# Convolution taps from PSUM, the triangles' inverse in PSUM, first values by segment, and x·sigmoid(x) as one activation

## The chip, the core and the metric

The kernel runs on one core of a Trainium2 chip. A core has five engines that run side by side, each through its own instructions in a fixed order: TensorE (PE) multiplies matrices, VectorE (DVE) and GpSimd (POOL) do elementwise work, ScalarE (ACT) applies functions, SyncE (SP) issues transfers. Engines wait for each other by semaphores. Data lie in SBUF (128 partitions) and in PSUM, whose banks hold 512 fp32 values a partition and take TensorE's results. The metric is the device time of one run in microseconds (us), lower is better.

## The reference

Two attention layers run over 1024 tokens and 256 context tokens, width 1024; a mixer block with an MLP runs on the 1024 tokens. Cut to what the change touches:

```python
# first block, each layer: modulation and gate
shift, scale, gate = split(silu(c) @ w_mod + b_mod, 3)
attn = rms_norm(o, subln_g) * (1 - lam_init)
x = x + gate * (concat([fourier_mix(a_in), pool_mix(b_in), attn]) * silu(g)) @ w_out

# second block: three branches from one projection of h
q_a = silu(a_q); o_a = gated_linear_attention(q_a, k_a, a_i, log_f_a)
qkv = silu(causal_short_conv(c_qkv, gdn_conv))      # 4 taps along time
m = eye(64) + where(strict, beta * (k @ k.T) * decay, 0)
sol = triangular_solve(m, rhs)                      # chunks of 64, unit diagonal
y = g0 * y_a + g1 * y_b + g2 * y_c;  x = x + rmsnorm(y @ w_out)
x = x + rmsnorm(square(relu(h @ w_up)) @ w_down)
```

## The kernel before

Tokens are cut into segments 0 and 1 (512 tokens each) and 2 (the context, 256). Every fp32 product is made of three matmuls on a high and a low part of both operands (lines 199 to 201, names `pp`, `h_hi`, `h_lo`, `whi`, `wlo`). A weight arrives as `wraw` by a DMA on SP's queue, ACT copies its high part (`whi`, line 177), POOL subtracts for the low part (`wlo`, line 178); there are 6 buffers of such pairs. A framework orders the instructions of every engine before the run and puts in the semaphores; the code's order sets priorities.

In layer 0 the modulation of the later steps (`mod`) is made while the Fourier projection runs: DVE adds up `w_mod` rows into `modacc` (lines 431, 433), TensorE sums over partitions into `modps` (line 437). The Fourier mixing itself goes through small products `mps` and `uvps`, DVE's additions into `uv` (line 1070) and the matmuls `eps`.

The mixer works on four pairs of heads p = 0 to 3 in pieces, whose code order stands in the tables MIX_FIRST, MIX and MIX_LAST: Av, Aq, Af, Ag project the first branch (`proj_tm` and `proj_fm`; each result goes to one of three `pp` banks and is evacuated by a callback), GA and GB are the two linear attentions, NA, NB, NC the output norms (line 1345), gA, gB, gC the gates `gs` (lines 1294 to 1299), Ck, Cq and Cv the convolved projections of the third branch (`conv`), I the triangles' inverse (`m_I`), U, Y, D what follows from it. `m_I` inverts 32 by 32 triangles, one per partition, by 31 steps on DVE: step i multiplies the rows known so far with a column (`tr`, line 1705) and sums (`ur`, line 1706). TensorE's `yp` product (line 1729) waits for the inverse. In `conv` ACT copies the product to `cv` and its scaled copy to `cvo` (lines 1602, 1604), DVE adds three shifted taps (line 1606), ACT takes the sigmoid (line 1608) and POOL multiplies (line 1609). Buffers named by `wt` (4 KB) come from a ring of 16, those by `wh` (2 KB) from a ring of 8.

Of the kernel before, what the change touches and what calls it, by code (L numbers as in the profile page):

```python
# [39 lines left out]
def shape_tables():  # L40
# [79 lines left out]
class Model:  # L120
# [130 lines left out]
    def setup(self):  # L251
# [5 lines left out]
        self.half = cp.tile([128, 1], F32, name="half")  # L257
        nc.gpsimd.memset(self.half, -0.5)
# [49 lines left out]
    def block1(self):  # L308
# [33 lines left out]
        sg = b1.tile([128, 8, 2], F32, name="sg")  # L342
# [68 lines left out]
    def mod(self, l, c0, sb, tp, bufs, add, tag="modps", depth=1):  # L411
# [4 lines left out]
        ps = tp.tile([128, 512], F32, tag=tag, name="modps", bufs=depth)  # L416
        pt = (ps if add else tp.tile([128, 512], F32, tag=tag, name="modpt", bufs=depth))[:, 0:8].rearrange("p (t two) -> p t two", two=2)
        if add:
            acc = sb.tile([128, 2, 512], F32, tag="modacc", name="modacc", bufs=2)
        for i in range(4):  # L420
            w = sb.tile([128, 2, 512], F32, tag="wmod", name="wmod", bufs=bufs)
            nc.sync.dma_start(out=w, in_=self.a["w_mod"][l, i * 256:(i + 1) * 256, c0:c0 + 512].rearrange("(k p) n -> p k n", p=128))
            for j in range(2):
# [4 lines left out]
                for c in range(2):  # L428
# [91 lines left out]
    def layer(self, l):  # L520
# [14 lines left out]

        def more(n=1):
# [85 lines left out]
        with ExitStack() as es:  # L622
            self.pp = self.pool("pp", bufs=4, space=PSUM, ctx=es)
            self.norm_pools(es, side="right")
            yp = self.pool("yp", ctx=es)
            for group in [(g,) for g in segs]:
                y = {}
                for g in group:
                    y[g] = [Tiles(e + t) for e, t in zip(early, self.load_y(yp, y_d, g, range(4, 8)))] if g == 0 else [Tiles(t) for t in self.load_y(yp, y_d, g, range(8))]
# [19 lines left out]
    def load_y(self, yp, y_d, g, ks, n=8, m=3):  # L649
# [4 lines left out]
        for k in ks:  # L654
            st = yp.tile([128, 512], F32, tag="yst", name="yst", bufs=m)[:, :ln]
# [73 lines left out]
    def attention(self, l, es, ak, ps_s, qk_d, v, g_d, y_d, upd):  # L729
# [139 lines left out]
        def step(i):  # L869
# [70 lines left out]
            def llast():  # L940
# [222 lines left out]
    def mixer(self, es):  # L1163
# [10 lines left out]
        self.g2_d = self.grid("g2_d", [128, 8, 128], 3, 8)  # L1174
        self.tri = mp.tile([128, 2, 128], F32, name="tri")
# [804 lines left out]
```

## Time and profile before

| what | value |
|---|---|
| median of 3 runs | 4307.32 us (4303.39 to 4315.31) |
| the profiled execution | 4301.6 us, span 4299.8 us |
| mean granted TensorE clock | 0.958 |
| PE busy | 3997.2 us, 93% of the span |
| DVE, ACT, POOL busy | 1926.8, 1528.3, 2005.0 us |

The span runs from the first to the last instruction. A share of busy time is a mean over stages with different limits: attention layer 0 lies before about 895 us, layer 1 before 1549 us, the mixer from 1563 to about 3500 us with four like periods of some 464 us, the MLP behind it. A busy PE at a lower granted clock takes longer for the same matmul.

### The profile page before, as it was taken

Reading aid. Unit: us, or ns where it says so; the run is one execution under the profiler, and the core shown is the slowest. Engines: PE = TensorE matmul, PEld = TensorE weight load, DVE = VectorE, ACT = ScalarE, POOL = GpSimd, SP = SyncE. Lnnn points to the kernel's source line nnn. Section 1 sums busy time; section 2 is a strip of 40 time slices with the busy share of each in tenths; the row PEclk is TensorE's granted clock in tenths of the full one; section 3 lists DMA queues with packets and bytes.
Section 4 is the critical chain, followed back from the end, with each engine's and each line's share of the span. In section 5 each row is a group of like instructions: output and inputs, shape, how many; then the busy total and the mean of one; then the engine's idle time right before and its main releaser. Section 6 shows DMA issues by size and latency. Waiting matters only on the chain.

```text
span 4299.8 us, 71521 instructions
## 1 busy us (share of the span) xinstructions
PE 3997.2 (93%) x28027; PEld 3445.3 (80%) x28027; DVE 1926.8 (45%) x3252; ACT 1528.3 (36%) x3256; POOL 2005.0 (47%) x2306
## 2 busy tenths in 40 slices
PE   6989999999999989999989898989989989999998
PEld 3878877788788778879879897979868877888886
DVE  3467376555347433464255623482258355122121
ACT  4221366433247433441224222341224134243332
POOL 2523122454312335564366536563566465445444
PEclk9989999999999999899999999999989889999999
DMA  6556321646422431222112221122112334334332
GB/s 217 166 176 201 124 83 46 202 146 177 164 76 75 135 89 43 70 67 66 56 53 61 65 66 55 46 68 68 50 41 62 94 120 159 96 98 132 99 96 83
DMA packets 372510, 429.20 MB, mean 100 GB/s; under 512 B 56743, under 2 KB 273341, under 8 KB 371917
## 3 DMA queue, kind: packets, MB, share of 16 engines
q1 hardware_dynamic: 283632, 294.60, 22.9%
q10 hardware_dynamic: 78620, 93.33, 6.8%
q0 software_dynamic: 9920, 36.70, 2.6%
q8 instruction: 220, 3.60, 0.3%
q14 instruction: 118, 0.96, 0.1%
HBM read 328.88 MB, written 95.64 MB: 99 GB/s over the span
## 4 chain that ended last, share of the span: by engine, by line
PE 57%; DVE 8%; POOL 4%; issue 4%; DMA 3%; ACT 2%; ACTq 1%; SPq 0%; DVEq 0%; POOLq 0%
PE pp L199 12%; PE pp L201 12%; PE pp L200 12%; PE dn L200 3%; PE dn L201 3%; PE dn L199 3%; DVE tr L1705 2%; PE o_ps L831 2%; DVE cvo L1606 1%; PE lv L1459 1%; PE t_ps L815 1%; DVE ur L1706 1%; POOL wlo L178 1%; PE s_ps L767 1%; PE s_ps L766 1%
## 5 line engine op out<-in xcount | busy, mean ns | idle before, releaser
L178 POOL TENSOR_TENSOR wlo<-wraw,whi 128x512 fp32r<-128x512 f32 x582 | 796.7, 1387 | 892.2 <-ACT whi L177 766.4
L199 PE MATMUL pp<-h_hi,whi 128*128 128x512 f32 (+1 forms) x2112 | 821.8, 390 | 34.6 <-ACT cvo L1604 16.3
L200 PE MATMUL pp<-h_lo,whi 128*128 128x512 f32 (+1 forms) x2112 | 815.0, 387 | 0.9 <-POOL h_lo L502 0.9
L201 PE MATMUL pp<-h_hi,wlo 128*128 128x512 f32 (+1 forms) x2112 | 811.2, 386 | 2.5 <-POOL wlo L178 2.5
L199 PE MATMUL pp<-whi,h_hi 128*128 128x256 f32 x2368 | 687.9, 292 | 35.5 <-ACT v L1431 14.0
L200 PE MATMUL pp<-wlo,h_hi 128*128 128x256 f32 x2368 | 687.0, 291 | 4.8 <-POOL wlo L178 4.8
L201 PE MATMUL pp<-whi,h_lo 128*128 128x256 f32 x2368 | 686.4, 290 | 0.0
L199 PEld LDWEIGHTS pp<-h_hi,whi 128*128 128x128 f32 x2112 | 404.5, 192 | 115.7 <-ACT cvo L1604 17.9
L199 PEld LDWEIGHTS pp<-whi,h_hi 128*128 128x128 f32 x2368 | 462.6, 196 | 40.1 <-ACT v L1431 14.2
L177 ACT ACTIVATE whi<-wraw 128x512 fp32r<-128x512 f32 x582 | 357.7, 625 | 374.0 <-PE pp L200 171.1
L200 PEld LDWEIGHTS pp<-wlo,h_hi 128*128 128x128 f32 x2368 | 464.0, 196 | 8.5 <-POOL wlo L178 6.5
L201 PEld LDWEIGHTS pp<-h_hi,wlo 128*128 128x128 f32 x2112 | 403.7, 191 | 81.7 <-POOL wlo L178 3.8
L200 PEld LDWEIGHTS pp<-h_lo,whi 128*128 128x128 f32 x2112 | 404.0, 191 | 76.1 <-POOL h_lo L502 1.2
L201 PEld LDWEIGHTS pp<-whi,h_lo 128*128 128x128 f32 x2368 | 462.5, 196 | 2.1
L787 DVE TENSOR_REDUCE mb<-s_ps 128x1 f32<-128x1280 f32 (+1 forms) x144 | 195.8, 1370 | 130.5 <-PE s_ps L767 128.4
L189 POOL TENSOR_TENSOR wlo<-wraw,whi 128x512 fp32r<-128x512 f32 x128 | 166.4, 1304 | 163.0 <-ACT whi L188 162.7
L200 PE MATMUL dn<-wlo,hid_hi 128*128 128x512 f32 x512 | 200.1, 391 | 0.0
L199 PE MATMUL dn<-whi,hid_hi 128*128 128x512 f32 x512 | 200.0, 391 | 0.0
L201 PE MATMUL dn<-whi,hid_lo 128*128 128x512 f32 x512 | 199.4, 391 | 0.0
L1606 DVE SCALAR_TENSOR_TENSOR cvo<-cv,vec,cvo 128x512 f32<-128x512 f32 x144 | 149.5, 1038 | 81.9 <-ACT cvo L1604 63.3
L796 ACT ACTIVATE p<-s_ps,mb 128x1280 f32<-128x1280 f32 x128 | 170.1, 1329 | 37.7 <-DVE mb L787 34.4
L1297 POOL TENSOR_TENSOR gs<-gs 128x256 f32<-128x256 f32 x96 | 76.2, 794 | 228.8 <-DVE gs L1296 226.5
(460 smaller groups left out, 7243.7 us busy)
## 6 DMA issues: line engine op xcount, KB each, us to landing
wraw<-in_w_in_dram SPq DMA_DIRECT2D x208, 256.0 KB
wraw<-in_w_up_dram SPq DMA_DIRECT2D x128, 256.0 KB
wraw<-in_w_down_dram SPq DMA_DIRECT2D x128, 256.0 KB
wraw<-in_w_out_dram SPq DMA_DIRECT2D x112, 256.0 KB
wraw<-in_w_in_dram SPq DMA_DIRECT2D x224, 128.0 KB
wmod<-in_w_mod_dram SPq DMA_DIRECT2D x48, 512.0 KB
qk<-qk_d POOLq DMA_DIRECT2D x16, 1280.0 KB, 6.7
g_d<-gs ACTq DMA_DIRECT2D x96, 128.0 KB
```

The source lines that it names most:

```text
L177: nc.scalar.activation(out=hi[:, :k, :o], in_=raw[:, :k, :o], func=AF.Copy)
L178: nc.gpsimd.tensor_tensor(out=lo[:, :k, :o], in0=raw[:, :k, :o], in1=hi[:, :k, :o].bitcast(F32), op=SUB)
L189: nc.gpsimd.tensor_tensor(out=lo, in0=raw, in1=hi.bitcast(F32), op=SUB)
L199: mm(ps, a[0], b[0], start=first, stop=False)
L200: mm(ps, a[0], b[1], start=False, stop=False)
L201: mm(ps, a[1], b[0], start=False, stop=last)
L787: V.tensor_reduce(out=b, in_=u.ps[m], axis=AX.X, op=MAX, negate=True)
L796: nc.scalar.activation(out=u.p[m], in_=u.ps[m], func=AF.Exp, bias=u.b[m], accum_out=u.s[m])
L831: mm(t.o_ps, v[k][:, t.hd * 128:t.hd * 128 + 128], t.parts[k // 4][:, k % 4], start=k == 0, stop=k == 9)
L1297: nc.gpsimd.tensor_tensor(out=t, in0=t, in1=sg[:, :, 128:256], op=MUL)
L1606: nc.vector.scalar_tensor_tensor(out=o, in0=r[:, 1 + j:513 + j], scalar=tap(j, f), in1=o, op0=MUL, op1=ADD)
L1705: V.tensor_tensor(out=tr[:, :n, :m], in0=ur[:, :n, :m], in1=mr[:, :m, i].unsqueeze(1).to_broadcast([128, n, m]), op=MUL)
```

## The change

Five edits. (1) `conv` keeps the product in its `pp` bank: the three shifted taps on DVE read the bank itself, an ACT copy `c_e` saves the last three columns of segment 0, and three narrow DVE taps add them at the start of segment 1. (2) The inverse `ur` lies in a PSUM bank, `tr` in a 2 KB buffer, and ACT copies the finished inverse to `us`, from which SP stores it; DVE instead of POOL sets its start values. (3) The first two projections of the mixer, Av and Aq of p = 0, are coded by segment (both load their weights twice: 8 more loads), and the mixer's constants are coded behind them. (4) Where sigmoid and a multiplication made x·sigmoid(x) (conv, Aq, gates of the layers, `sc`), one Silu activation stands. The gain `sub_gain` moves from the gate into `norm_apply`. (5) `mod` is cut in two stages: the sums on DVE, and TensorE's product with what follows it; `more` finishes one group's second stage when it starts the next group.

By the orders of both kernels, DVE loses 16 products of Aq, 40 of the gates and 2 of `sc`; its 144 taps of 128x512 become 144 on 511, 510 or 509 columns that read PSUM, and 72 of 1 to 3 columns. ACT loses 48 `cv` copies and 48 sigmoids, and gains 48 Silu, 24 `c_e`, 4 `us`, 8 `whi` and 19 table loads (36 before, 55 now). POOL loses 48 products and 48 small copies or memsets, and gains 8 `wlo`. PE's matmuls are as many as before.

```diff
-MIX_FIRST = "Av+"
+MIX_FIRST = "Av Aq Av Aq"
...
-        self.half = cp.tile([128, 1], F32, name="half")
-        nc.gpsimd.memset(self.half, -0.5)
+        self.half = self.ind[:, 4:5]
...
         for j, nm in enumerate(("c", "c_ctx")):
-            nc.scalar.activation(out=sg[:, :, j], in_=self.vec[nm], func=AF.Sigmoid)
-            nc.vector.tensor_tensor(out=self.sc[:, :, j], in0=sg[:, :, j], in1=self.vec[nm], op=MUL)
+            nc.scalar.activation(out=self.sc[:, :, j], in_=self.vec[nm], func=AF.Silu)
...
+    def mod_stages(self, l, c0, sb, tp, bufs, add, tag="modps", depth=1):
...
+        yield
+        pt = tp.tile([128, 512], F32, tag=tag, name="modpt", bufs=depth)[:, 0:8].rearrange("p (t two) -> p t two", two=2)
         if add:
...
         def more(n=1):
-            for c in left[:n]:
-                with self.tc.issue_after(self.mark.ins):
-                    self.mod(*c, mw, tp, 5, True, "fo", 5)
-            del left[:n]
+            for _ in range(n):
+
+                while open_:
+                    next(open_.pop(), 0)
+                if left:
+                    with self.tc.issue_after(self.mark.ins):
+                        open_.append(self.mod_stages(*left.pop(0), mw, tp, 5, True, "fo", 5))
+                        next(open_[0])
...
                 def evac_g(f, g, ps):
                     off, ln = SEG[g]
                     sg = gp.tile([128, 512], F32, tag="sg", name="sg", bufs=2)[:, :ln]
-                    nc.scalar.activation(out=sg, in_=ps, func=AF.Sigmoid)
-                    if wb < 2:
-                        nc.vector.tensor_tensor(out=sg, in0=sg, in1=ps, op=MUL)
-                    else:
-                        nc.vector.scalar_tensor_tensor(out=sg, in0=sg, scalar=self.sub_gain[:, l:l + 1], in1=ps, op0=MUL, op1=MUL)
+                    nc.scalar.activation(out=sg, in_=ps, func=AF.Silu)
...
-            yp = self.pool("yp", ctx=es)
+
+            ysp, xnp, yp = (self.pool(n, ctx=es) for n in ("ys", "xn", "yp"))
...
-        self.nc.vector.tensor_tensor(out=o, in0=o, in1=ps[:, 2:4].rearrange("p a b -> p (a b)"), op=MUL)
+        self.nc.vector.scalar_tensor_tensor(out=o, in0=o, scalar=gain, in1=ps[:, 2:4].rearrange("p a b -> p (a b)"), op0=MUL, op1=MUL)
...
+        for name in MIX_FIRST.split():
+            self.piece("m_", name, 0)
+        self.mixer_constants(mp)
...
         def ev(f, g, ps):
             s = slice(512 * g, 512 * g + 512)
-            nc.scalar.activation(out=q[f][:, s], in_=ps, func=AF.Sigmoid)
-            nc.vector.tensor_tensor(out=q[f][:, s], in0=q[f][:, s], in1=ps, op=MUL)
-
-        self.proj_fm([self.W[:, 256 * p:256 * p + 256]], self.h, (0, 1), ev)
+            nc.scalar.activation(out=q[f][:, s], in_=ps, func=AF.Silu)
+
+        if p == 0:
+            return self.by_segment(lambda segs: self.proj_fm(cols, self.h, segs, ev))
+        self.proj_fm(cols, self.h, (0, 1), ev)
+
+    def by_segment(self, f):
+
+        for g in (0, 1):
+            f((g,))
+            yield
...
         def evac(f, g, ps):
-            r = raw[f, g] = self.wh("cv", [128, 516])
-            if g == 0:
-                nc.gpsimd.memset(r[:, 0:4], 0.0)
-            else:
-                nc.gpsimd.tensor_copy(out=r[:, 0:4], in_=raw[f, 0][:, 512:516])
-            nc.scalar.activation(out=r[:, 4:], in_=ps, func=AF.Copy)
             o = out[f][:, 512 * g:512 * g + 512]
             nc.scalar.activation(out=o, in_=ps, func=AF.Copy, scale=tap(3, f))
-            for j in range(3):
-                nc.vector.scalar_tensor_tensor(out=o, in0=r[:, 1 + j:513 + j], scalar=tap(j, f), in1=o, op0=MUL, op1=ADD)
-            sg = self.wh("sg")
-            nc.scalar.activation(out=sg, in_=o, func=AF.Sigmoid)
-            nc.gpsimd.tensor_tensor(out=o, in0=o, in1=sg, op=MUL)
+            if g == 0:
+                last[f] = self.st("c_e", [128, 3], bufs=2)
+                nc.scalar.activation(out=last[f], in_=ps[:, 509:512], func=AF.Copy)
+            for d in range(1, 4):
+                V.scalar_tensor_tensor(out=o[:, d:], in0=ps[:, 0:512 - d], scalar=tap(3 - d, f), in1=o[:, d:], op0=MUL, op1=ADD)
+            if g:
+                for d in range(1, 4):
+                    V.scalar_tensor_tensor(out=o[:, :d], in0=last[f][:, 3 - d:], scalar=tap(3 - d, f), in1=o[:, :d], op0=MUL, op1=ADD)
+            nc.scalar.activation(out=o, in_=o, func=AF.Silu)
...
         mr = self.wt("mr", [128, 32, 32])
-        ur = self.wt("ur")[:, :512].rearrange("p (j i) -> p j i", i=32)
-        tr = self.wt("tr")[:, :512].rearrange("p (j i) -> p j i", i=32)
-        G.memset(ur, 0.0)
+        ur = self.op_.tile([128, 16, 32], F32, tag="o", name="ur")
+        us = self.wh("us", [128, 16, 32])
+        tr = self.wh("tr", [128, 16, 32])
+        V.memset(ur, 0.0)
...
+        nc.scalar.activation(out=us, in_=ur, func=AF.Copy)
         for e in range(2):
-            nc.sync.dma_start(out=ud.rearrange("h c b (j two) i -> two (h c b) j i", two=2)[e], in_=ur[64 * e:64 * e + 64])
+            nc.sync.dma_start(out=ud.rearrange("h c b (j two) i -> two (h c b) j i", two=2)[e], in_=us[64 * e:64 * e + 64])
...
-                    xt = gp.tile([128, D], F32, tag="fx", name="fx", bufs=4)
+                    xt = (self.wt("y0") if t % 2 else gp.tile([128, D], F32, tag="fx", name="fx", bufs=2))
```

**Layer 0, behind the gate's projection, PE.** Before; `modps` is the modulation, `mps` and `uvps` the Fourier part:

```order
L437 MATMUL modps<-ind,modacc 128x1 x4
L1060 MATMUL mps<-mid,wc 128x2
L1066 MATMUL uvps<-wc,eo 128x128 x6
L437 MATMUL modps<-ind,modacc 128x1 x4
L1066 MATMUL uvps<-wc,eo 128x128 x2
L1060 MATMUL mps<-mid,wc 128x2
L1066 MATMUL uvps<-wc,eo 128x128 x2
L1060 MATMUL mps<-mid,wc 128x2
L1066 MATMUL uvps<-wc,eo 128x128 x8
L1060 MATMUL mps<-mid,wc 128x2
L1066 MATMUL uvps<-wc,eo 128x128 x2
L437 MATMUL modps<-ind,modacc 128x1 x8
```

After, at the same place:

```order
L202 MATMUL pp<-h_hi_148,wlo 128x256
L1073 MATMUL uvps<-wc,eo 128x128 x2
L1067 MATMUL mps<-mid,wc 128x2
L1073 MATMUL uvps<-wc,eo 128x128 x8
L1067 MATMUL mps<-mid,wc 128x2
L1073 MATMUL uvps<-wc,eo 128x128 x2
L441 MATMUL modpt<-ind,modacc 128x1 x4
L200 MATMUL eps<-whi,uv 128x256
L201 MATMUL eps<-wlo,uv 128x256
```

The small Fourier products stood behind the first `modps`; now they stand in front of the one row of modulation left here (eight of them, with two `mps`, further ahead, among the gate's last matmuls). Four more columns of `modpt` come 23 matmuls into `eps`, the rest later.

**Start of the mixer, ACT.** Before, from the second segment's normalised activations (`h_hi<-ntt`) on; `v` evacuates the first values:

```order
L516 ACTIVATE h_hi_13400<-ntt 128x512 x8
L1176 DMA tri<-in_tri_dram 128x256
L1178 DMA dmin<-in_dmin_dram 128x128
L1180 DMA lvmask<-in_lvmask_dram 128x192
L1184 DMA gain_14361<-in_hgrn_onorm_dram 128x128
L1184 DMA gain_14363<-in_gla_onorm_dram 128x256
L1184 DMA gain_14365<-in_gdn_onorm_dram 128x128
L1186 DMA ab<-in_gdn_a_log_dram 128x8
L1187 DMA ab<-in_gdn_dt_bias_dram 128x8
L1195 ACTIVATE lbe<-lbp 128x8
L1431 ACTIVATE v<-pp 128x128 x6
```

After; `v` of segment 0 first, and weights between the `h_hi`:

```order
L1460 ACTIVATE v_14326<-pp 128x128
L1460 ACTIVATE v_14327<-pp 128x128
L1460 ACTIVATE v_14326<-pp 128x128
L1460 ACTIVATE v_14327<-pp 128x128
L1460 ACTIVATE v_14326<-pp 128x128
L1460 ACTIVATE v_14327<-pp 128x128
L178 ACTIVATE whi<-wraw 128x512
L520 ACTIVATE h_hi_13363<-ntt 128x512
L178 ACTIVATE whi<-wraw 128x512
L520 ACTIVATE h_hi_13363<-ntt 128x512
L178 ACTIVATE whi<-wraw 128x512
L1460 ACTIVATE v_14326<-pp 128x128
```

The six evacuations of segment 0 moved ahead of `h_hi` and of eight constant loads, and seven `whi` stand among the `h_hi`; the constants come after the first `aq`.

**Inverse of p = 1, ACT.** Before, at the end of the convolutions; `gs` are the next gates, `whi` weights of the coming projections:

```order
L1299 DMA g_d_2_14333<-gs 128x2x128
L1294 ACTIVATE gs<-pp 128x512
L1299 DMA g_d_2_14333<-gs 128x2x128
L177 ACTIVATE whi<-wraw 128x512 x3
L1294 ACTIVATE gs<-pp 128x512
L177 ACTIVATE whi<-wraw 128x512
L1620 ACTIVATE sqt<-cvo 128x512
L1299 DMA g_d_2_14333<-gs 128x2x128
L1294 ACTIVATE gs<-pp 128x512
L1620 ACTIVATE sqt<-cvo 128x512
```

After:

```order
L1310 ACTIVATE gs<-pp 128x512
L1315 DMA g_d_2_14304<-gs 128x2x128
L1310 ACTIVATE gs<-pp 128x512
L1315 DMA g_d_2_14304<-gs 128x2x128
L178 ACTIVATE whi<-wraw 128x512
L1735 ACTIVATE us<-ur 128x512
L178 ACTIVATE whi<-wraw 128x512 x2
L1310 ACTIVATE gs<-pp 128x512
L178 ACTIVATE whi<-wraw 128x512
L1647 ACTIVATE sqt<-cvo 128x512 x2
L1315 DMA g_d_2_14304<-gs 128x2x128
L1310 ACTIVATE gs<-pp 128x512
```

The copy `us` waits for the inverse, and `whi` rows that did not stand behind it now do.

## Rows read from the trace of the kernel before

**Rows 1.** Page: busy time; the core's clock; the chain that ended last.

```profile
PE 3997.2 (93%) x28027; PEld 3445.3 (80%) x28027; DVE 1926.8 (45%) x3252; ACT 1528.3 (36%) x3256; POOL 2005.0 (47%) x2306
...
core 0: 4299.8 us, clock 0.958
...
PE 57%; DVE 8%; POOL 4%; issue 4%; DMA 3%; ACT 2%; ACTq 1%; SPq 0%; DVEq 0%; POOLq 0%
```

**Rows 2.** Busy time by stretch: start:end, length, engines, TensorE's clock, DMA share, GB/s.

```profile
286.00:318.00 32.00, 19.76 (x125) 19.12 (x124) 31.13 (x61) 7.02 (x16) 6.39 (x4) 0.73 0.59 184
1549.00:1568.00 19.00, 4.99 (x27) 4.80 (x26) 11.70 (x22) 6.46 (x16) 0.00 (x0) 0.64 0.16 31
1453.00:1462.00 9.00, 5.40 (x15) 4.19 (x15) 2.50 (x5) 1.89 (x3) 2.27 (x8) 0.62 0.89 291
1915.00:1985.00 70.00, 58.39 (x418) 54.55 (x416) 53.94 (x104) 15.82 (x28) 40.19 (x34) 0.88 0.21 54
2380.00:2440.00 60.00, 48.25 (x316) 45.33 (x315) 54.66 (x98) 16.21 (x29) 33.47 (x28) 0.86 0.22 55
2845.00:2905.00 60.00, 48.45 (x320) 45.63 (x319) 54.19 (x96) 15.67 (x29) 34.11 (x29) 0.86 0.22 57
3275.00:3320.00 45.00, 40.88 (x240) 36.77 (x238) 42.49 (x78) 10.46 (x19) 23.65 (x28) 0.95 0.23 55
```

**Rows 3.** Timeline, layer 0: start, length, instruction, idle before and releaser.

```profile
301.19 1.84 PE L437 MATMUL modps<-ind,modacc 128*128 128x1 f32 x8 [11.18 <-DVE modacc L433]
...
316.71 0.36 PE L199 MATMUL eps<-whi,uv 128*128 128x256 f32 x1
...
296.99 7.36 DVE L433 SCALAR_TENSOR_TENSOR modacc<-wmod,sc,modacc 128x512 f32<-128x512 f32 x11
```

**Rows 4.** Timeline, start of the mixer, PE and then ACT.

```profile
1563.25 0.58 PE L199 MATMUL pp<-whi,h_hi 128*128 128x256 f32 x1 [14.01 <-ACT v L1431]
...
1558.17 1.29 ACT L516 ACTIVATE h_hi<-ntt 128x512 fp32r<-128x512 f32 x2 [1.42 <-DVE ntt L515]
1558.89 0.34 ACTq L1176 DMA_DIRECT2D tri<-in_tri_dram  x1
...
1562.78 1.10 ACT L1431 ACTIVATE v<-pp 128x128 f32<-128x128 f32 x6
```

**Rows 5.** Busy time of line 1705 alone (`tr`) in the four inverse stretches, 31 products each.

```profile
sum 235.00, DVE 95.84; mean DVE 23.96
```

**Rows 6.** Lines: count, duration in ns as min/median/max, first and last start.

```profile
L1705 DVE TENSOR_TENSOR tr<-ur,mr x124: 147/702/2333, 1918.7 to 3314.0; 128x2 f32<-128x2 f32 x4, 128x3 f32<-128x3 f32 x4, 128x8 f32<-128x8 f32 x4, 128x10 f32<-128x10 f32 x4
...
L1345 DVE SCALAR_TENSOR_TENSOR o<-o,on_rs,gt x64: 335/342/2423, 1914.5 to 3441.5; 128x128 f32<-128x128 f32 x64
...
L1606 DVE SCALAR_TENSOR_TENSOR cvo<-cv,vec,cvo x144: 736/752/2293, 1853.4 to 3329.0; 128x512 f32<-128x512 f32 x144
...
L637 DVE SCALAR_TENSOR_TENSOR xn<-pp,mods,xn x40: 469/740/751, 784.4 to 1538.9; 128x512 f32<-128x512 f32 x32, 128x256 f32<-128x256 f32 x8
...
L1608 ACT ACT_TABLE_LOAD  x8: 1283/1283/1283, 1871.5 to 3245.5; - x8
```

**Rows 7.** PE's waits from 2375 to 2445 us: total, times, longest.

```profile
PE pp L199 <- ACT cvo L1604: 6.0, 2, 5.7
PE pp L199 <- ACT whi L177: 4.9, 1, 4.9
```

**Rows 8.** Timeline, second inverse, PE and then ACT.

```profile
2387.97 0.79 PE L199 MATMUL pp<-h_hi,whi 128*128 128x512 f32 x1 [5.67 <-ACT cvo L1604]
...
2396.07 0.28 PE L199 MATMUL pp<-whi,h_hi 128*128 128x256 f32 x1
2396.19 0.28 PE L200 MATMUL pp<-wlo,h_hi 128*128 128x256 f32 x1
...
2426.70 1.67 ACT L177 ACTIVATE whi<-wraw 128x512 fp32r<-128x512 f32 x3 [5.82 <-POOL gs L1298]
```

**Rows 9.** Page, the costliest groups: the conv taps, with busy time and mean ns.

```profile
L1606 DVE SCALAR_TENSOR_TENSOR cvo<-cv,vec,cvo 128x512 f32<-128x512 f32 x144 | 149.5, 1038 | 81.9 <-ACT cvo L1604 63.3
```

More of the change, by code (lines that the diff above doesn't have):

```diff
@@ L88, in shape_tables @@
     ind[:, 2:4] = 1
+    ind[:, 4] = -0.5
     for n, L in enumerate((TX, TC)):
@@ L409, in load_x, with mod @@
             nc.scalar.activation(out=sq, in_=st, func=AF.Square, accum_out=ss[:, i:i + 1])
-    def mod(self, l, c0, sb, tp, bufs, add, tag="modps", depth=1):
+    def mod(self, *args):
+        for _ in self.mod_stages(*args):
+            pass
+    def mod_stages(self, l, c0, sb, tp, bufs, add, tag="modps", depth=1):
         nc = self.nc
         V = nc.vector
-        ps = tp.tile([128, 512], F32, tag=tag, name="modps", bufs=depth)
-        pt = (ps if add else tp.tile([128, 512], F32, tag=tag, name="modpt", bufs=depth))[:, 0:8].rearrange("p (t two) -> p t two", two=2)
-        if add:
+        if not add:
+            ps = tp.tile([128, 512], F32, tag=tag, name="modps", bufs=depth)
+        else:
             acc = sb.tile([128, 2, 512], F32, tag="modacc", name="modacc", bufs=2)
@@ L628, in layer @@
                 for g in group:
[L629 removed]
+                    y[g] = [Tiles(e + t) for e, t in zip(early, self.load_y(yp, y_d, g, range(4, 8), sp=ysp))] if g == 0 else [Tiles(t) for t in self.load_y(yp, y_d, g, range(8), sp=ysp)]
                 xk = {g: [None] * 8 for g in group}
@@ L944, in llast @@
                 for e, j, a in each():
-                    if j >= first(a) and self.norm_apply(*a, st["ps"], j - first(a), y_d):
+                    if j >= first(a) and self.norm_apply(*a, self.sub_gain[:, l:l + 1], st["ps"], j - first(a), y_d):
                         ends.remove(e)
@@ L1174, in mixer, with mixer_constants @@
         self.g2_d = self.grid("g2_d", [128, 8, 128], 3, 8)
+        self.W = W
+        self.heads = [dict(y=[None, None], parts=set(), yt={}) for _ in range(4)]
+        self.running = {}
+        self.mo = {}
+        self.np_, self.npp = self, self
+        self.depth = 1
+        for name in MIX_FIRST.split():
+            self.piece("m_", name, 0)
+        self.mixer_constants(mp)
+        end = 1 + max(i for i, n in enumerate(MIX_LAST.split()) if n not in LAST)
+        for p, order in zip(range(4), (MIX, MIX, MIX, MIX_LAST)):
+            for i, name in enumerate(order.split()):
+                if p == 3 and i == end:
+                    mq_es.close()
+                    self.fp = self.pool("hid0", side="right")
+                q = p + name.endswith("+")
+                if name in LAST:
+                    if self.stop != "mixer":
+                        self.piece("o_", name)
+                elif 0 <= q < 4:
+                    self.piece("m_", name.strip("+"), q)
+        assert all(next(r, self) is self for r in self.running.values() if r)
+    def mixer_constants(self, mp):
+        nc, a = self.nc, self.a
         self.tri = mp.tile([128, 2, 128], F32, name="tri")
@@ L1200, in mixer @@
         nc.vector.tensor_scalar(out=self.lb[:, 1], in0=self.lb[:, 0], scalar1=-1.0, scalar2=1.0, op0=MUL, op1=ADD)
-        self.W, self.ab = W, ab
-        self.heads = [dict(y=[None, None], parts=set(), yt={}) for _ in range(4)]
-        self.running = {}
-        self.mo = {}
-        self.np_, self.npp = self, self
-        self.depth = 1
-        end = 1 + max(i for i, n in enumerate(MIX_LAST.split()) if n not in LAST)
-        for p, order in zip(range(-1, 4), (MIX_FIRST, MIX, MIX, MIX, MIX_LAST)):
-            for i, name in enumerate(order.split()):
-                if p == 3 and i == end:
-                    mq_es.close()
-                    self.fp = self.pool("hid0", side="right")
-                q = p + name.endswith("+")
-                if name in LAST:
-                    if self.stop != "mixer":
-                        self.piece("o_", name)
-                elif 0 <= q < 4:
-                    self.piece("m_", name.strip("+"), q)
-        assert all(next(r, self) is self for r in self.running.values() if r)
+        self.ab = ab
     def piece(self, kind, name, *args):
@@ L1398, in m_Av @@
     def m_Av(self, p):
-        self.heads[p]["av"] = self.values(self.W[:, 2048 + 256 * p:2048 + 256 * p + 256])
+        cols = self.W[:, 2048 + 256 * p:2048 + 256 * p + 256]
+        if p:
+            self.heads[p]["av"] = self.values(cols)
+            return
+        v = self.heads[p]["av"] = [self.wt("v0", [128, 8, 128]) for _ in range(2)]
+        return self.by_segment(lambda segs: self.values(cols, v, segs))
     def m_GA(self, p, f):
@@ L1423, in m_GB, with values @@
         return self.gla(h["bqk"][0], z, h["bqk"][1], h["bv"], o)
-    def values(self, cols):
-        v = [self.wt("v", [128, 8, 128]) for _ in range(2)]
+    def values(self, cols, v=None, segs=(0, 1)):
+        v = v or [self.wt("v", [128, 8, 128]) for _ in range(2)]
         def evac(t, ps):
@@ L1585, in conv @@
     def conv(self, p, part):
-        nc = self.nc
+        nc, V = self.nc, self.nc.vector
         out = [self.wt("cvo") for _ in range(2)]
-        raw = {}
+        last = {}
         c0 = 7184 + 1024 * part + 256 * p
```

21 lines of the change are left out of this document (12 added, 9 removed).

## The prediction

> **What bounds the kernel now.** I read the page first: TensorE is busy for 93% of the span, and 57% of the chain that ended last is its work, with DVE at 8% as the next engine [rows 1]. So work taken from ACT, POOL or DVE is worth only what TensorE waits for it. TensorE's idle time is 4299.8 − 3997.2 = 302.6 us, and the mean clock of 0.958 costs up to 0.042 × 4300 = 180 us more. Then I looked for the stretches that the change touches, and in which TensorE both pauses and runs at a lower clock [rows 2]. There are seven. In layer 0, behind the gate's projection, TensorE works 19.76 of 32 us while DVE works 31.13: DVE is the bound there. At the mixer's start TensorE works 4.99 of 19 us. At the output projection of layer 1 it works 5.40 of 9 us. In the four stretches of the triangles' inverse it lacks 235 − 195.97 = 39 us in all, at a clock of 0.86 to 0.95, and in the second and third DVE works 54 of 60 us. In each the clock fell to the lower level after TensorE had paused. The clock's loss in the inverse stretches is (1 − clock) × length: 8.4 + 8.4 + 8.4 + 2.2 = 27 us.
>
> **The change part by part.** *Start of the mixer.* TensorE stops for 14.01 us because ACT has not evacuated the first values: the six copies of segment 0 stand behind the last `h_hi` (1558.17) and eight constant loads issued from 1558.89 on, and run at 1562.78 [rows 4]. The change puts these six in front, and the matmuls of Aq on segment 0 behind them: 48 of 128x512, at twice the 0.12 us from one start of a 128x256 matmul to the next [rows 8], so 11.5 us of work that needs nothing of segment 1. The gap of 14.0 us can go, and the clock's loss of 0.36 × 19 = 6.8 us with it. On the other side the chain to the last `h_hi` gets seven weight copies between, and the constants' loads are only moved. The bounds are 0 (the next stop is as long) and −21; nearest to the gap itself I take −15.
>
> *Layer 0.* TensorE waits 11.18 us for DVE's sums at the first `modps`, and only then runs the small Fourier products; `eps` starts at 316.71 [rows 3]. Now these run in front. DVE was busy all the time, so the gain is what DVE does before `eps` and now does later or not at all: the third group's sums, 11 instructions of the kind that takes 7.36 / 11 = 0.67 us [rows 3], are 7.4 us; three or four gate products, as large, that became Silu are some 2 us. The start of `eps` moves to about 307, and the low clock over these 20 us (0.27 × 32 = 8.6 us) shrinks by a few us. What is late next is the remaining modulation, which nobody needs before the output projection. Bounds 0 and −20; I take −13.
>
> *The four inverses.* Here two things change on DVE. The 31 products `tr` of an inverse take 95.84 / 4 = 24.0 us [rows 5], and the same shape takes very different times (147 to 2333 ns over all shapes) [rows 6]; if each shape took the fastest of its four times, worked out shape by shape, the four sums would be 60.9 us, so 8.7 us less per inverse. The conv taps show the same tail with one shape: from 736 ns to 2293 ns, mean 1038 [rows 6, 9]. The trace has the like instruction with one operand in PSUM: line 637, 40 times, at most 751 ns [rows 6]. The tail is missing there, and so I expect it to be gone for `ur` and the taps in PSUM. Twelve taps within an inverse's stretch then save 12 × 0.29 = 3.5 us and the narrow ones add 1. DVE's 54.7 us become about 43. The `ur` reductions, which read only `tr`, I leave as they are.
>
> What does TensorE get of these 11 us? In the second stretch it waits 5.7 us for an ACT scaled copy that stands behind DVE's output norm, and 4.9 us for weights that ACT copies late, since the gate `gs` ahead of them was held up [rows 7, 8]. The first of these waits is hardly touched, since the buffer that ACT waits for is still freed by DVE. The second can go. But the order now gives TensorE less to do beside the inverse: ahead of `yp` of p = 1 stand 215 projection matmuls of 128x256 in place of 289, 74 less at 0.12 us [rows 8], which is 9 us. So it comes to `yp` 9 us earlier and the inverse ends 11 earlier: the time gained there is a shift of work, and the yield is what TensorE's idle time and low clock lose. Of 39 + 27 = 66 us over four stretches I take half, −32; the bounds are −66 and +30 (the loss below).
>
> *Output projection of layer 1.* `pp` matmuls now stand ahead of the norm's transposes. Of the 3.6 us without work and 0.38 × 9 = 3.4 us of clock I take −4 (0 to −7).
>
> *Table loads.* 19 more at 1.283 us [rows 6] are 24.4 us on ACT, which is busy 36% [rows 1] and 16 of 60 us in an inverse's stretch [rows 2]. The cover is that idle time; where a load stands in front of an evacuation that TensorE waits for, it counts. I expose a quarter: +6 (0 to +24). [...]
>
> *The rest* I cost at nothing. POOL's 48 products and DVE's 58 go, off TensorE's path; the 36 gain products are as wide as before; `us` is four short copies on ACT, and delays only if the inverse is late (below); 8 more weight loads come in a stretch where DMA works 16% of the time [rows 2]; the MLP's buffer and `half` change no wait that I see.
>
> The sum is −15 − 13 − 32 − 4 + 6 = −58: 4301.6 becomes 4243.6. The profiled run is 5.7 us below the median of 4307.32, so I forecast a median of 4248.
>
> **The rivals.** *The inverses give nothing back* (chance 0.22). For it speaks that TensorE reaches `yp` with 9 us less of cover, about what DVE saves, and that the 5.7 us wait stays. Then −15 − 13 − 4 + 6 = −26, and the median is 4281.
>
> *Slower, by the hold on PSUM banks and the copy `us`* (chance 0.10). A conv product now keeps one of the three `pp` banks until DVE has done its three taps. TensorE fills a bank in 24 × 0.24 = 5.8 us, so a bank may be held 11.5 us after its product; DVE's 16 output norm products of one p stand in a row in front of taps, 16 × 0.342 = 5.5 us without the tail that reaches 2.4 us [rows 6], with three taps of 0.74 for each of two banks behind them: 10 to 12 us. On ACT, `us` stands before two of the next weight copies: if the inverse ends later than TensorE's work lasts, weights come late too. From some 10 us of lateness per period it decides. Priced at 10 us more of idle and 3 of clock in each of four stretches, in place of −32 there are +52, and with exposed loads (+12) the sum is −15 − 13 − 4 + 52 + 12 = +32, and the median 4339. With half of the price, +26 and +6, the sum is 0 and the median 4307, no change. [...]
>
> *Larger* (0.15): all idle and low clock of the inverses goes, −66 for −32, so the sum is −92 and the median 4215.
>
> *Little moves* (0.05): TensorE's pauses only shift to the next wait, in the mixer's start and layer 0 too: −5, 4302.
>
> **How the numbers follow.** My forecast, with its own range of 4230 to 4268, has 0.48; with 0.22 + 0.10 + 0.15 + 0.05 that is 1. About 13 us (0.3%) is what a measurement can tell from no change, so faster ends at 4294. The range has to leave out 2 in 10: half of the slower rival, some of the larger and of the last. It goes from 4205 to 4296. Faster: 0.48 + 0.15 + most of 0.22 = 0.83; same: 0.09, from the last rival and from the slower one at half its price; slower: 0.08.
>
> **What would show it.** Right: no wait of TensorE over 5 us between 1548 and 1570 us of the old time line; `eps` about 10 us earlier; the slowest `tr` and tap below 0.8 us, DVE at some 43 us in an inverse's stretch; TensorE's clock there above 0.9. Wrong: a wait of `pp` on DVE's taps, of weights on ACT behind `us`, or of `yp` on the inverse that is longer than 10 us; 55 table loads with TensorE waiting behind many of them; or taps that keep a tail over 2 us.

## The result and the profile after

The changed kernel takes 4233.71 us (median of 4 runs, 4231.04 to 4239.46), the kernel before 4305.35 us beside it: a ratio of 0.9834, 95% interval 0.981 to 0.9857, 71.6 us less. The forecast was 4248, 59 us under the median of 4307.32 then on record.

The page of the changed kernel, busy times and chain, and the core's clock:

```profile
PE 3966.4 (94%) x28027; PEld 3421.8 (81%) x28027; DVE 1846.1 (44%) x3278; ACT 1540.2 (36%) x3263; POOL 1905.7 (45%) x2205
...
core 0: 4229.3 us, clock 0.966
...
PE 29%; DVE 2%; DMA 1%; POOL 1%; ACT 0%; issue 0%; DVEq 0%; ACTq 0%; SPq 0%; POOLq 0%
```

The chain that ended last, followed back from the end, covers only a third of the span here (its shares sum to 33%), so it is not compared with the one before. Against [rows 1] TensorE's idle time fell from 302.6 to 262.9 us, and the same 28027 matmuls were busy 30.8 us shorter, because the clock rose (0.958 to 0.966; in the changed kernel a matmul of 128x512 starts 0.43 us behind the one before from 2340.19 to 2342.32 us, at a clock of 0.50, and 0.23 us behind it from 2344.42 on, at 1.00): 70.5 us together. To see where, the time line is cut at the same matmuls in both kernels. Busy time by stretch of the kernel before (start:end, length, PE, PEld, DVE, ACT, POOL, clock, DMA share, GB/s); the rows are the later half of layer 0's projections with the start of attention, the mixer's start, the four periods from the end of the second linear attention to the next first one, and the MLP:

```profile
267.00:527.70 260.70, 243.44 (x1496) 220.32 (x1495) 157.97 (x282) 60.66 (x117) 62.52 (x52) 0.94 0.50 163
1498.90:1623.20 124.30, 110.29 (x584) 95.68 (x583) 41.61 (x63) 40.91 (x81) 51.03 (x51) 0.95 0.28 82
1852.70:2167.60 314.90, 298.16 (x2152) 268.21 (x2154) 140.32 (x266) 94.64 (x244) 157.05 (x159) 0.96 0.23 64
2319.20:2631.80 312.60, 295.02 (x2114) 265.45 (x2112) 142.88 (x265) 92.92 (x240) 155.71 (x159) 0.96 0.24 64
2777.00:3088.50 311.50, 294.06 (x2112) 265.09 (x2114) 143.33 (x263) 95.02 (x244) 155.99 (x161) 0.96 0.25 69
3183.50:3586.50 403.00, 361.73 (x2562) 315.66 (x2561) 208.30 (x369) 134.94 (x316) 226.30 (x246) 0.91 0.31 92
3586.50:4299.80 713.30, 687.78 (x3029) 566.05 (x3027) 169.05 (x202) 245.84 (x424) 361.67 (x283) 0.98 0.33 105
```

The same stretches of the changed kernel:

```profile
267.50:523.00 255.50, 241.99 (x1496) 217.48 (x1494) 146.81 (x258) 60.21 (x117) 64.97 (x52) 0.96 0.51 167
1494.10:1602.30 108.20, 108.20 (x585) 93.83 (x583) 42.58 (x59) 48.68 (x92) 63.04 (x59) 1.00 0.39 114
1831.80:2131.60 299.80, 289.31 (x2154) 261.97 (x2155) 127.01 (x283) 96.11 (x243) 128.28 (x134) 0.98 0.25 68
2282.30:2584.60 302.30, 290.88 (x2113) 263.23 (x2111) 127.13 (x281) 95.13 (x239) 128.16 (x134) 0.97 0.24 66
2731.20:3029.80 298.60, 287.28 (x2117) 260.97 (x2116) 126.48 (x280) 95.12 (x242) 128.01 (x135) 0.98 0.26 72
3124.30:3513.10 388.80, 350.20 (x2562) 306.43 (x2561) 190.10 (x390) 136.75 (x316) 197.15 (x219) 0.94 0.33 98
3513.10:4229.30 716.20, 688.86 (x3029) 566.74 (x3027) 169.40 (x202) 245.59 (x424) 361.01 (x283) 0.98 0.32 103
```

The lengths differ by −5.2, −16.1, −15.1, −10.3, −12.9, −14.2 and +2.9 us; what lies between them adds 0.4. At the mixer's start TensorE is now busy in all of 108.20 us at the full clock (1.00). The four periods give 52.5 us: 21.2 of TensorE's idle time, and 31.3 of its busy time for almost the same matmuls, which is the clock (0.91 to 0.96 before, 0.94 to 0.98 after).

The instructions of the inverse and the taps after, as [rows 6] (lines have moved: 1733 is `tr`, 1632 the taps, 1361 the output norm):

```profile
L1733 DVE TENSOR_TENSOR tr<-ur,mr x124: 146/404/1136, 1894.4 to 3237.9; 128x2 f32<-128x2 f32 x4, 128x3 f32<-128x3 f32 x4, 128x8 f32<-128x8 f32 x4, 128x10 f32<-128x10 f32 x4
...
L1632 DVE SCALAR_TENSOR_TENSOR cvo<-pp,vec,cvo x144: 666/742/753, 1832.0 to 3259.4; 128x511 f32<-128x511 f32 x48, 128x510 f32<-128x510 f32 x48, 128x509 f32<-128x509 f32 x48
...
L1361 DVE SCALAR_TENSOR_TENSOR o<-o,on_rs,gt x64: 336/340/2487, 1876.3 to 3369.5; 128x128 f32<-128x128 f32 x64
```

The tail is gone from the taps and from `tr` (60.32 us in all, 95.84 in [rows 5]); the output norm, which reads SBUF twice, keeps it, and so do the 72 narrow taps, which read `c_e` and `cvo` in SBUF (168 ns to 1854). The second period's wait, in which [rows 7] had two, from 2328 to 2393 us of the changed kernel (total, times, longest):

```profile
PE pp L200 <- DVE cvo L1632: 7.3, 1, 7.3
PE yp L1758 <- DVE T L1753: 1.3, 1, 1.3
```

and what stood before it in the time line, on PE, DVE and POOL:

```profile
2339.60 0.79 PE L200 MATMUL pp<-h_hi,whi 128*128 128x512 f32 x1 [7.26 <-DVE cvo L1632]
...
2325.17 10.49 DVE L1361 SCALAR_TENSOR_TENSOR o<-o,on_rs,gt 128x128 f32<-128x128 f32 x16 [0.84 <-POOL on_rs L155]
2335.59 0.73 DVE L1632 SCALAR_TENSOR_TENSOR cvo<-pp,vec,cvo 128x510 f32<-128x510 f32 x1
2336.24 1.85 DVE L1635 SCALAR_TENSOR_TENSOR cvo<-c_e,vec,cvo 128x2 f32<-128x2 f32 x1
...
2329.49 2.44 POOL L1363 TENSOR_TENSOR y<-y,o 128x1024 f32<-128x1024 f32 x1 [1.81 <-DVE o L1361]
2331.88 2.58 POOL L179 TENSOR_TENSOR wlo<-wraw,whi 128x512 fp32r<-128x512 f32 x2
...
2335.74 2.34 POOL L1363 TENSOR_TENSOR y<-y,o 128x1024 f32<-128x1024 f32 x1 [1.18 <-DVE o L1361]
```

The wait for weights (4.9 us) is gone. The other one stayed and changed its name: TensorE waits for a bank whose taps stand behind the output norm's 16 products on DVE, which took 10.49 us (7.41 before, from 2379.79), and behind a narrow tap of 1.85 us that ends with POOL's `y`.

### The profile page after: what moved, and what is told of

Read it like the earlier page. It is cut to its first block, busy times and chain, and to the rows that moved or that the text cites. A ratio compares the mean times of both kernels' runs of the same rounds, so it can differ in the third digit from the quotient of the medians.

```text
span 4229.3 us, 71442 instructions
## 1 busy us (share of the span) xinstructions
PE 3966.4 (94%) x28027; PEld 3421.8 (81%) x28027; DVE 1846.1 (44%) x3278; ACT 1540.2 (36%) x3263; POOL 1905.7 (45%) x2205
## 5 line engine op out<-in xcount | busy, mean ns | idle before, releaser
L200 PE MATMUL pp<-h_hi,whi 128*128 128x512 f32 (+1 forms) x2112 | 824.7, 391 | 47.3 <-DVE cvo L1632 26.6
L200 PE MATMUL pp<-whi,h_hi 128*128 128x256 f32 x2368 | 679.3, 288 | 0.0
L803 ACT ACTIVATE p<-s_ps,mb 128x1280 f32<-128x1280 f32 x128 | 170.0, 1328 | 32.3 <-DVE mb L794 31.5
L1310 ACT ACTIVATE gs<-pp 128x512 f32<-128x512 f32 x96 | 57.4, 597 | 335.6 <-PE pp L202 333.1
```

The costliest lines, as they stand in the source:

```text
L200: mm(ps, a[0], b[0], start=first, stop=False)
L803: nc.scalar.activation(out=u.p[m], in_=u.ps[m], func=AF.Exp, bias=u.b[m], accum_out=u.s[m])
```

## The experiments

Each was timed beside the kernel before; the differences below are against those runs of it.

| kernel | median us | ratio, 95% interval | difference us | the four sums of `tr`, us |
|---|---|---|---|---|
| the changed kernel | 4233.71 | 0.9834 (0.981 to 0.9857) | −71.6 | 60.32 |
| inv_sbuf | 4243.55 | 0.9868 (0.9837 to 0.9898) | −61.4 | 68.77 |
| taps_alone | 4262.23 | 0.9901 (0.9879 to 0.9923) | −38.7 | 94.45 |
| silu_alone | 4261.19 | 0.9901 (0.9882 to 0.9921) | −39.7 | 75.42 |
| both_old | 4285.42 | 0.9961 (0.9948 to 0.9974) | −17.6 | 95.97 |
| conv_sbuf | 4272.94 | 0.9936 (0.9911 to 0.9961) | −32.0 | |
| conv_sbuf_ring | 4275.86 | 0.9941 (0.9922 to 0.996) | −27.1 | |
| conv_old | 4304.46 | 1.0003 (0.999 to 1.0015) | −0.4 | |
| conv_old_ring | 4296.84 | 0.9988 (0.9975 to 1.0) | −6.2 | 57.19 |
| conv_old_usdve | 4291.46 | 0.9974 (0.9964 to 0.9984) | −9.4 | |
| mods_one | 4240.45 | 0.9862 (0.9831 to 0.9894) | −64.5 | |
| nb_after_I | 4232.82 | 0.9839 (0.9821 to 0.9858) | −70.2 | |
| nb_U2 | 4223.31 | 0.9816 (0.9797 to 0.9835) | −77.6 | 60.24 |

**The inverse back in SBUF** (inv_sbuf).

```diff
-        ur = self.op_.tile([128, 16, 32], F32, tag="o", name="ur")
+        ur = self.wt("ur")[:, :512].rearrange("p (j i) -> p j i", i=32)
```

> The changed kernel with the inverse `ur` back in an SBUF buffer; everything else, the copy `us` too, stays. Theory: the place of `ur` frees DVE from POOL, so that with two SBUF operands `tr` gets its long times back. POOL has less to do than before (27 of 62 us in an inverse's stretch against 34 of 60), so the four sums of `tr` go from 60.3 us to some 75 to 90, an inverse's chain from 38.5 to 42 to 46 us, and the time up by 10 to 25 us, to 4244 to 4259. Rival: the shorter chain comes from POOL's products having gone, not from PSUM; then `tr` stays under 66 us and the time within 5 us of 4234.

4243.55, 10 us more by the differences, though the intervals overlap. The time is at the theory's lower end; `tr`, at 68.77 us, is little above the rival's 66 and far below 95.97. So in this order PSUM takes only the last 8.5 us off `tr`; most of the saving is there with `ur` in SBUF. The second inverse takes 40.0 us from first to last, against 39.0 in the changed kernel; 10 us of time do not follow from that, and they are likely, not shown.

**Taps from SBUF copies, Silu kept** (conv_sbuf).

```diff
+            r = last[f, g] = self.wh("cv", [128, 516])
...
+            nc.scalar.activation(out=r[:, 4:], in_=ps, func=AF.Copy)
...
-                V.scalar_tensor_tensor(out=o[:, d:], in0=ps[:, 0:512 - d], scalar=tap(3 - d, f), in1=o[:, d:], op0=MUL, op1=ADD)
+                V.scalar_tensor_tensor(out=o, in0=r[:, 1 + j:513 + j], scalar=tap(j, f), in1=o, op0=MUL, op1=ADD)
```

> The changed kernel with the taps reading the SBUF copy `cv` again (copy by ACT, four columns by POOL), Silu kept. Theory: reading PSUM removes the taps' long times but holds the banks, and TensorE now waits 5 to 7 us a period for DVE's taps behind the output norm; without the hold that wait goes or becomes one on ACT's scaled copy of about the same length, while the taps' mean goes from 0.74 to 0.9 us or more and the inverse's chain grows by 1 to 3 us. The time goes to 4236 to 4250. Rival: the hold costs more than the long times, and the time falls below 4225.

4272.94: neither. TensorE stopped once in each of the first three periods for 27 to 28 us, longer than any wait of either kernel.

**The whole old convolution** (conv_old): the edit above, and

```diff
-            nc.scalar.activation(out=o, in_=o, func=AF.Silu)
+            sg = self.wh("sg")
+            nc.scalar.activation(out=sg, in_=o, func=AF.Sigmoid)
+            nc.gpsimd.tensor_tensor(out=o, in0=o, in1=sg, op=MUL)
```

> The changed kernel with the whole convolution as before: SBUF copies, sigmoid on ACT, the product on POOL. Against the run that has only the SBUF copies this adds POOL's 48 products. Theory: they contend with DVE's two-operand SBUF work but not with `tr`, whose operand is in PSUM, so `tr` stays at 60 to 64 us and the taps' mean goes to 1.0 us; the time to 4240 to 4260. Rival: the gain in the four inverses is that of the conv edits alone; then the time is at least 4270.

4304.46, no faster than the kernel before: by its number the rival's range, but with stops of 27 to 32 us that neither had.

**The same two with `tr` and `us` in the 4 KB ring** (conv_sbuf_ring, conv_old_ring).

```diff
-        us = self.wh("us", [128, 16, 32])
-        tr = self.wh("tr", [128, 16, 32])
+        us = self.wt("us")[:, :512].rearrange("p (j i) -> p j i", i=32)
+        tr = self.wt("tr")[:, :512].rearrange("p (j i) -> p j i", i=32)
```

> As the run with taps from SBUF copies and Silu, but `tr` and `us` come from the ring of 4 KB buffers, not from the ring of eight 2 KB buffers that the copies `cv` need. Theory: the stop of 27 us of TensorE in each inverse's stretch of that run came from the ring (the copies for Cq could not start before `us` gave its buffer back), not from the taps; with the ring relieved it falls below 10 us and the time to 4236 to 4258: what is then left over 4234 is the price of taps in SBUF by themselves. Rival: the taps in SBUF cost it themselves; the stop stays over 20 us and the time near 4273.

> As the run with the whole convolution of before, with `tr` and `us` in the 4 KB ring: the inverse in PSUM and all the rest of the change, without the conv edit. Theory: without the stop of 32 us a period the time falls from 4304 to 4250 to 4275; POOL's products make it 8 to 20 us slower than the run with Silu. Rival: it stays above 4290, since the old convolution as such is what costs.

4275.86 and 4296.84: the theory of the ring fell, the stops stayed, and the times are the rivals'. The time line of conv_sbuf_ring, PE and then ACT, shows what they wait for:

```profile
2388.20 0.79 PE L200 MATMUL pp<-h_hi,whi 128*128 128x512 f32 x1 [27.36 <-ACT cvo L1633]
...
2386.98 0.60 ACT L1735 ACTIVATE us<-ur 128x512 f32<-128x512 f32 x1 [24.70 <-DVE ur L1734]
2387.47 1.84 ACT L1633 ACTIVATE cvo<-pp,vec 128x512 f32<-128x512 f32 x3
```

`us` waits for the inverse 24.7 us, and three evacuations of Cq's products, for which TensorE waits, stand behind it on ACT. In the order of the changed kernel they come ahead of `us`.

**Both as before** (both_old): the old convolution and the old inverse, all else of the change.

> The changed kernel with both the convolution and the inverse as before; left of the change are the start of the mixer, the modulation's stages, the gates' Silu and the rest. Theory: it keeps what the first 1623 us of the old time line gained, 21 us, and nothing of the periods: 4280 to 4288. Rival: edits outside the convolution and the inverse (Aq's Silu, buffers) also shorten the periods; then it is below 4270.

4285.42, as the theory said. From the mixer's first products on, its matmuls run 19 to 23 us ahead of the kernel before, and neither gain nor lose in the periods. All that the periods gain comes from the convolution and the inverse.

**Silu alone** (silu_alone) and **taps in PSUM alone** (taps_alone), each added to both_old:

```diff
-            sg = self.wh("sg")
-            nc.scalar.activation(out=sg, in_=o, func=AF.Sigmoid)
-            nc.gpsimd.tensor_tensor(out=o, in0=o, in1=sg, op=MUL)
+            nc.scalar.activation(out=o, in_=o, func=AF.Silu)
```

```diff
-            nc.scalar.activation(out=r[:, 4:], in_=ps, func=AF.Copy)
...
-                V.scalar_tensor_tensor(out=o, in0=r[:, 1 + j:513 + j], scalar=tap(j, f), in1=o, op0=MUL, op1=ADD)
...
+                V.scalar_tensor_tensor(out=o[:, d:], in0=ps[:, 0:512 - d], scalar=tap(3 - d, f), in1=o[:, d:], op0=MUL, op1=ADD)
```

> The run with the old convolution and the old inverse, with one thing of the conv edit: Silu in place of sigmoid on ACT and product on POOL; the taps stay in SBUF. Theory: `tr` in SBUF is slow while POOL works on SBUF beside it, and POOL's products are a good part of that work; without them the four sums of `tr` fall from 96.0 us to 68 to 80, and the time from 4285 to 4255 to 4272. Rival: the tail of `tr` goes only when the taps leave SBUF or `ur` does; the sums stay over 88 us and the time within 6 us of 4285.

> The run with the old convolution and the old inverse, with the other thing of the conv edit: taps that read PSUM; sigmoid and POOL's product stay. Theory: the taps go to at most 0.76 us, `tr` keeps 85 to 96 us since POOL's products remain, and the hold of the banks costs a wait of 5 to 8 us a period; the time is 4270 to 4288. Rival: it is the taps that free DVE and with it TensorE; the time falls to 4255 or less.

Silu alone takes `tr` from 95.97 to 75.42 us and the time down by 39.7 − 17.6 = 22 us: the theory. The taps alone leave `tr` at 94.45, as expected, and yet gain 21 us, more than the theory and less than the rival: the time lies between. This gain did not come through a shorter inverse: the second one takes 49.1 us from first to last, and 48.8 in both_old. In that run TensorE's waits for ACT went; that the 48 `cv` copies taken off ACT are the reason is likely, and was not tried by itself. From 1780 to 3500 us, in both_old, silu_alone and taps_alone (total, times, longest):

```profile
PE pp L200 <- ACT cvo L1633: 26.1, 11, 5.7
PE pp L200 <- ACT whi L178: 14.4, 3, 4.9
...
PE yp L1756 <- DVE T L1751: 15.0, 4, 6.7
PE pp L200 <- ACT whi L178: 8.5, 5, 3.3
PE pp L200 <- ACT cvo L1633: 3.9, 2, 1.9
...
PE pp L200 <- DVE ur L1735: 20.7, 3, 7.2
PE pp L200 <- ACT whi L178: 0.8, 2, 0.4
```

With Silu 28 us of waits for ACT went, with the taps 40; waits for DVE came, 12 us more for `yp` in the one and 20.7 for a bank in the other. The second inverse became 4.7 us shorter with Silu (44.1), and TensorE now waits for it (`yp`); how much of the 22 us came by the inverse and how much by ACT's work was not separated. Together (inv_sbuf, which keeps the copy `us` and DVE's start values too) the two gain 61.4 − 17.6 = 44 us, so they add up.

**`us` on DVE** (conv_old_usdve), in conv_old_ring:

```diff
-        nc.scalar.activation(out=us, in_=ur, func=AF.Copy)
+        V.tensor_copy(out=us, in_=ur)
```

> The run with the old convolution and the inverse in PSUM, with the copy `us` made by DVE, not by ACT. Theory: TensorE's stop of 27 to 32 us a period in the two runs before came from `us`, which stood on ACT ahead of the scaled copies of Cq's products and waited there for the inverse; off ACT the stop falls below 12 us and the time from 4297 to 4260 to 4280. Rival: the stop stays, since DVE's taps of Cq stand behind the whole inverse in its own queue; then the time stays at 4285 to 4300.

4291.46: the rival. The stop of 31.5 us broke up into 4.5 and 22.5: DVE has Cq's taps behind the whole inverse in its queue. ACT's `us` was only the first thing in the way.

**The modulation in one stage** (mods_one): `more` calls `mod` whole, and the tile `modps` is taken before the sums, as in the kernel before.

> The changed kernel with the modulation in one stage again. Theory: the 13 us that `eps` gained in layer 0 are given back within the kernel, since what starts behind it (attention's first softmax, the output projection) waits for others; then `eps` comes 10 to 13 us later, but the time goes up by only 0 to 5 us, to 4234 to 4239. Rival: the 13 us are kept, and another edit of the layers loses some 10 us; then the time goes to 4244 to 4248.

4240.45 and 7.1 us more by the differences, between the two; the intervals overlap. `eps` came 7.6 us later than in the changed kernel, and the difference is kept.

**NB later** (nb_after_I, nb_U2).

```diff
-... CP0 CP1 NB Cv I Cq U0 gA0+ CQ0 D0 D0
+... CP0 CP1 Cv I Cq NB U0 gA0+ CQ0 D0 D0
```

```diff
-... CP0 CP1 NB Cv I Cq U0 gA0+ CQ0 D0 D0
+... CP0 CP1 Cv I Cq U0 gA0+ CQ0 NB D0 D0
```

> The changed kernel with the output norm NB coded behind Cq in the first three periods, not ahead of Cv. TensorE's wait of 6.5 to 7.3 us a period for DVE's taps stands behind NB's 16 products on DVE (10.5 us in the second period). Theory: the wait goes, with the low clock behind it some 9 us a period, but the products now stand in the inverse's chain and make it 5 to 6 us longer, so the net is 0 to 5 us a period and the time 4219 to 4234. Rival: the inverse's end decides, not the wait, and the time goes up by 5 to 18 us.

> The changed kernel with NB coded behind CQ0 in the first three periods, so that its 16 products on DVE stand neither ahead of Cv's last taps nor inside the inverse's chain. Theory: both the wait of TensorE for the taps (7 us a period) and the longer chain of the run with NB behind Cq are avoided; 5 to 9 us a period, 4207 to 4220. Rival: the products now stand ahead of DVE's work on the state of the third branch, for which TensorE waits as long; 4230 to 4240.

4232.82: the wait went, but the inverse now took 47.3 us from first to last, against 39.0 in the changed kernel, and the sum is nothing, as expected. 4223.31 for nb_U2, the fastest median here and 3 us above the range that the theory gave: the inverse takes 39.2 us, and TensorE waits for `yp`, in the second period 4.3 us:

```profile
PE yp L1758 <- DVE T L1753: 4.3, 1, 4.3
```

It is 6 us faster than the changed kernel by the differences; the intervals overlap, so this is likely, not shown.

## Why the prediction was right, and where it was not

*Mixer's start, −15, and output projection, −4.* Right. The stop of 14.01 us is gone. The same 19 us from 1549 on in the changed kernel, beside [rows 2]:

```profile
1549.00:1568.00 19.00, 19.00 (x124) 17.42 (x123) 11.70 (x18) 11.20 (x23) 9.79 (x9) 1.00 0.48 137
```

The gain is 16.1 us here and 4 at the output projection. Whether the cut by segment or the later constants did it was not separated.

*Layer 0, −13.* Right as to `eps`, which started at 303.05, 13.7 us earlier than [rows 3]. The step that failed is the next one, that the modulation is all that is late behind it: of this lead 4.7 us are left at 523 us, and 0.9 at 1300 (the same matmuls in both kernels). Undoing the stages costs 7.1 us. The start of attention gives back 5 us. In the time line of the changed kernel, the softmax's first steps on ACT and the product that waits for them:

```profile
456.98 0.63 ACT L666 ACTIVATE y_hi<-yst 128x512 fp32r<-128x512 f32 x1 [9.81 <-DMA yst<-y_d]
457.62 1.28 ACT L803 ACT_TABLE_LOAD   x1
458.92 1.33 ACT L803 ACTIVATE p<-s_ps,mb 128x1280 f32<-128x1280 f32 x1
...
460.39 0.79 PE L773 MATMUL s_ps<-qk 128*128 128x512 f32 x1 [3.51 <-ACT p L803]
```

The first `s_ps` came 9.7 us earlier than before; ACT had a copy for the output projection in front of its softmax, which waited for a transfer, and then a table load. The three stand so in the kernel before too, 7.7 us later, with a wait of 1.6 us there. So 2 of the 5 us are this wait; the clock, 0.95 from 449 to 523 us and 1.00 in the like stretch before, accounts for most of the rest. What was late next stood on ACT, and I had looked on TensorE and DVE alone. Other edits of the layers cost a few us more, for at the output projection of layer 0 the run without the stages was 7.7 us behind the kernel before; which of them was not tried.

*The inverses, −32.* This is the term that was mis-sized: from both_old to the changed kernel it is 71.6 − 17.6 = 54 us. In the four stretches themselves I had counted 66 us of idle time and low clock and taken half. But the clock rose in the whole period: of 52.5 us in the rows above 31.3 are clock, where the term held 27 / 2 = 13.5. In the last period alone TensorE's busy time shrank by 11.5 us, most of it behind the inverse.

The step on DVE came out in size: `tr` at 60.32 us for 60.9, the inverse's chain 39.0 us from first to last in the second period for 49.0. That TensorE's gain comes through it holds for a part only: the taps alone gained 21 us with the chain as long as before, when TensorE's waits for ACT's weights and scaled copies went. The prediction left the first of its two waits in the second stretch as hardly touched, and of the second said only that it can go. The reason given for the tail was half right. I put the tail down to operands in SBUF. The runs show that POOL belongs to it: with POOL's products gone and `ur` still in SBUF, `tr` fell from 95.97 to 75.42, and with the taps in PSUM as well to 68.77. They show that PSUM is enough too: conv_old_ring keeps POOL's products, and `tr` from PSUM took 57.19 us, less than the 60.9 that the shortest of each shape add up to in the kernel before. In the changed kernel none of the 124 took over 1.11 times the shortest of its shape, though 43 lay beside POOL's work by more than 0.1 us. Two rows of the kernel before show the two engines together, DVE and then POOL:

```profile
2387.49 2.17 DVE L1705 TENSOR_TENSOR tr<-ur,mr 128x3 f32<-128x3 f32 x1
...
2387.28 2.37 POOL L1347 TENSOR_TENSOR y<-y,o 128x1024 f32<-128x1024 f32 x1 [1.80 <-DVE tr L1705]
```

A product of 3 columns lasts 2.17 us and ends with POOL's instruction (at 2389.66 and 2389.65), which is the output norm's and stays in the changed kernel. Of the 144 taps before, 48 took over 1.15 times the shortest, and POOL worked during 96% of their time on the mean (from the start and length of each record); 39 that were not long lay beside its work too, so not every overlap costs; after, 59 of the 144 lay beside POOL's work by more than 0.1 us and none was long.

That the order gives TensorE 9 us less to do beside the inverse did little harm: `yp` waits 1.3 us at most.

*The signs.* The taps stay below 0.8 us (753 ns). For `tr` that sign could not come: its largest shape, 128x512, takes 1.03 us at the shortest before and 1.10 after. DVE was not at 43 us: from 2330 to 2392 it worked 51.08 of 62 us, with part of the norm's 10.49 in it. The clock there was 0.92, as forecast.

*Table loads, +6.* There are 55, as read from the order, and no wait of TensorE over 5 us ends on one. ACT's busy time rose by 12 us in all. A load costs its row, 1.28 us, and no more in this stretch of the time line of the changed kernel:

```profile
1681.14 1.28 ACT L1581 ACT_TABLE_LOAD   x1
1682.44 0.26 ACT L1581 ACTIVATE ds_e<-ds_e 128x64 f32<-128x64 f32 x1
1682.71 1.28 ACT L1582 ACT_TABLE_LOAD   x1
```

The next activation starts 0.02 us behind the load, and the next load as closely behind it; for 41 of the 55 loads it starts no more than 0.03 us behind. The term was not tried by itself.

*The sum.* By the trace the terms are −16 and −4 at the mixer's start and the output projection, −1 for the layers, −52.5 for the periods and +3 for the MLP, which had none. The forecast counted 12 us too much in layer 0 and 20 too little in the periods, and 6 us for loads that the trace doesn't show; that it came within 15 us of the median is in part luck.

*The rivals.* The hold on the banks came, by a norm that kept its tail (10.5 us, where 5.5 had been worked out without it), and TensorE waits 5.2 to 7.3 us a period for it, but it took the place of the wait of 5.7 us and was not added to it. The copy `us` on ACT did the harm that was feared, 27 us a stop, only in kernels whose taps read SBUF copies. With the whole old convolution the inverse in PSUM makes both_old 11 us slower (−6.2 against −17.6), and in the changed kernel it seems to make it about 10 faster (inv_sbuf; the intervals overlap). Why the order puts Cq's work behind the inverse in the former and not in the changed kernel is open.

## What to carry to other kernels

A two-operand product on VectorE whose duration has a long tail is worth a look at what GpSimd does at the same moment: take one operand from PSUM, or take the work off GpSimd; here the first alone took `tr` from 95.97 to 57.19 us, and the second to 75.42. That is not yet time: the kernel with 57.19 was slower than the one with 95.97, by what stood behind the inverse in the queues. When a wait is removed, count the low clock behind it as well, in the whole stage (here 31.3 of the periods' 52.5 us), and look on every engine for the wait that comes next. Undoing one edit of several can cost more than it brought, since a new order decides; run each edit alone as well.

## What the runs showed that I had not expected

GpSimd's 48 products of about 1.3 us, which TensorE never waited for by more than 1.4 us, cost some 22 us of the kernel's time together with the sigmoids before them: `tr` on VectorE got 20.6 us shorter without them, and TensorE's waits for ACT fell. And the copy of an inverse on ACT, 0.6 us long, had three evacuations queued behind it, for which TensorE stopped for 27 us; in the one kernel where the copy was moved away, 22.5 of 31.5 us of such a stop stayed in one piece, behind VectorE's queue. Last, the taps in PSUM gained as much as Silu, with the inverse no shorter.
